# A diffusion backbone on one core: all large SBUF tiles start at multiples of 4096 bytes

## The chip, the cores and the metric

The kernel runs on one core of a Trainium2 chip. The metric is device time in microseconds (us) of one launch. SBUF is the core's working memory: 128 partitions, each with its own row of bytes, and a tile takes the same byte range of every partition. "Offset" means here the byte in a partition at which a tile begins, and "offset modulo 4096" how far past a multiple of 4096 that is.

## The reference

Two layers, each of three sub-layers, run over 256 latent tokens and 256 context tokens of width 1024. Cut to what matters:

```
for l in range(2):
    m = silu(c) @ w_ada[l] + b_ada[l]              # 9 rows of 1024: shift, scale, gate per sub-layer
    x = LN(ALPHA*x + gate * 0.5 * swiglu(modulate(x), ff1_gate, ff1_up, ff1_down))
    h = modulate(x)
    y = concat(neighbourhood_attention(h), rg_lru(h), fourier_mix(h)) @ w_out[l]
    x = LN(ALPHA*x + gate * y)
    x = LN(ALPHA*x + gate * 0.5 * swiglu(modulate(x), ff2_gate, ff2_up, ff2_down))
```

The hidden width of the two feed-forward blocks (FFN) is 2816, and all tensors are float32. Latent and context tokens share all weights. Output: the latent stream, 256 x 1024.

## The kernel before

The activations stand transposed in SBUF, features in the partitions and tokens in the columns: context tokens are columns 0 to 255 and latent tokens 256 to 511. `xT` is the residual stream (8 chunks of 128 features x 512 tokens), `hH` and `hL` the modulated input as a high and a low part, `aH` and `aL` the same for the hidden layer or for the concatenated heads. Splitting into two parts keeps accuracy with the fast matmul type float32r: each product is the sum of three matmuls, high weight x high input, low weight x high input, high weight x low input.

A weight unit is 128 output columns of one matrix over up to 8 blocks of 128 inputs. `issue` (lines 229 to 255) starts its DMA on SyncE's queue into one of five `raw` tiles; each partition receives up to eight pieces of 512 bytes. `use_one` (L257) then has ScalarE cast `raw` to `whi` (L271) and VectorE, at times GpSimd, subtract to get `wlo` (`split_lo`, L583). `mmh` (L383) records every matmul of the projections, in two halves of 256 tokens. The program's names of PSUM targets tell the stage: `gu` is gate and up of an FFN, `dn` its down projection, `pj` the mixer's input projection, `head` the projections that start a sub-layer while its input is still being normalised, `wo` the mixer's output projection, `adat` a small matmul (2 columns) that turns a row of the modulation into columns, `gate` the gates of the recurrence.

The modulation of later sub-layers is computed beside the FFNs by VectorE (`acc`, `fold`, L293 to L299), from `w_ada` blocks that come through the same `raw` tiles. The start (L1209 to L1300) loads `x` and the context into `in` tiles, turns them into `xT` (`xtp`, L1260), and computes the first modulation on TensorE (`adap`, L310). The order of all instructions is written out in the program (nothing is reordered by a scheduler), and each engine runs its own list, waiting on semaphores for the others.

Where tiles lie follows from the order in which they are asked for. The pool `const` holds single tiles, one after the other; behind it follow the pools `wraw` (5 `raw` tiles), `whi`, `wlo` (5 each), `acc` (6), `scr` (13 scratch tiles of 2048 bytes: `s`, `sg`, `pr`, `h32`, ...), `sm` and `dv` (small ones). Every size is rounded up to 32 bytes. The first tile of `const` begins at byte 16512, which is 128 past a multiple of 4096.

Of the kernel before, what the change touches and what calls it, by code (L numbers as in the profile page):

```python
# [11 lines left out]
F32 = mybir.dt.float32  # L12
# [7 lines left out]
DEPTH = 2  # L20
D = 1024
KD = D // 128
# [43 lines left out]
def kernel(ctx: ExitStack, tc: tile.TileContext, x, cx, vecs, cst, bias, w_ada,  # L66
# [3 lines left out]
    const = ctx.enter_context(tc.tile_pool(name="const", bufs=1))  # L70
# [10 lines left out]

    V, S, G, PE = nc.vector, nc.scalar, nc.gpsimd, nc.tensor

    xT = const.tile([128, KD, 512], F32, name="xT")
    hH = const.tile([128, KD, 512], F32R, name="hH")
    hL = const.tile([128, KD, 512], F32R, name="hL")
    aH = const.tile([128, 8, 512], F32R, name="aH")
    aL = const.tile([128, 8, 512], F32R, name="aL")
    cs = const.tile([128, 1408], F32, name="cs")
    ident = cs[:, 0:128]  # L90
    bdC = cs[:, 128:256]
# [1 line left out]
    CN = cs[:, 384:896].rearrange("p (a b) -> p a b", a=2)  # L93
    SN = cs[:, 896:1408].rearrange("p (a b) -> p a b", a=2)
    vT = const.tile([128, V_ROWS], F32, name="vT")
    onesD = const.tile([128, 128], F32, name="onesD")
    one_c = const.tile([128, 1], F32, name="one_c")
    pick = const.tile([128, 2, 2], F32, name="pick")
    scol = const.tile([128, KD, 2], F32, name="scol")
    join = const.tile([128, 2], F32, name="join")  # L100
    bmean = const.tile([128, 6], F32, name="bmean")
    kcol = const.tile([128, 8], F32, name="kcol")
    lbd = const.tile([128, 8, 128], F32, name="lbd")
    fbd = const.tile([128, 2, 128], F32, name="fbd")
    AB = const.tile([128, 2, 2, 128], F32, name="AB")
    scol_z = AB[:, 0].rearrange("p a (k s) -> p (a k) s", s=32)
    mcol = [const.tile([128, 2, 72], F32, name=f"mcol{l}") for l in range(DEPTH)]

    def vcol(name, i, n=1):
        o = V_OFF[name] + i  # L110
# [2 lines left out]
    def s512(nm):  # L113
        return scr.tile([128, 512], F32, tag="s", name=nm)
# [32 lines left out]
    for l in range(DEPTH):  # L147
        p = {}
# [644 lines left out]
    def fno_weights():  # L793
        for c in range(2):
            t = mps("fab")
            PE.matmul(t[:, 0:128], lhsT=bdC, rhs=fbd[:, c], start=True, stop=True)
            PE.matmul(t[:, 128:256], lhsT=bdS, rhs=fbd[:, c], start=True, stop=True)
            S.copy(AB[:, c].rearrange("p a f -> p (a f)"), t[:, 0:256])

# [17 lines left out]
    def mixer(l, both, nm, tl, nxt):  # L817
# [115 lines left out]
        def t_fa(pool, i):  # L933
            t = pool("fa")
            for c in range(2):
                PE.matmul(t[:, c * 256:(c + 1) * 256], lhsT=fT[c][:, i * 128:(i + 1) * 128],
                          rhs=AB[:, c].rearrange("p a f -> p (a f)"), start=True, stop=True)
            fa[i] = s512("fas")
# [461 lines left out]
```

## Time and profile before

| | |
|---|---|
| median of 3 runs | 1828.69 us (1824.31 to 1830.50) |
| the profiled execution | 1825.6 us, span 1823.8 us, mean granted TensorE clock 0.983 |
| TensorE matmul busy | 1746.8 us (96% of the span), 14241 matmuls |
| VectorE busy | 1208.9 us (66%) |
| ScalarE busy | 700.3 us (38%) |
| GpSimd busy | 194.8 us (11%) |
| DMA | 253.33 MB, 139 GB/s in the mean |

Matmuls overlap each other, so a matmul's own duration is longer than its share of the time; the pace is read from how many start in a stretch. The profile names an instruction by its line, engine, and output<-inputs, with buffer numbers left out. The chain of work that ended last is followed back from the last instruction and says which engine the time depended on.

### The profile page before, as it was taken

Reading aid. Unit: us, or ns where it says so; the run is one execution under the profiler, and the core shown is the slowest. Engines: PE = TensorE matmul, PEld = TensorE weight load, DVE = VectorE, ACT = ScalarE, POOL = GpSimd, SP = SyncE. Lnnn points to the kernel's source line nnn. Section 1 sums busy time; section 2 is a strip of 40 time slices with the busy share of each in tenths; the row PEclk is TensorE's granted clock in tenths of the full one; section 3 lists DMA queues with packets and bytes.
Section 4 is the critical chain, followed back from the end, with each engine's and each line's share of the span. In section 5 each row is a group of like instructions: output and inputs, shape, how many; then the busy total and the mean of one; then the engine's idle time right before and its main releaser. Section 6 shows DMA issues by size and latency. Waiting matters only on the chain.

```text
span 1823.8 us, 33834 instructions
## 1 busy us (share of the span) xinstructions
PE 1746.8 (96%) x14241; PEld 1693.7 (93%) x14241; DVE 1208.9 (66%) x1918; ACT 700.3 (38%) x1119; POOL 194.8 (11%) x207
## 2 busy tenths in 40 slices
PE   6999999999989999999999999999999988979997
PEld 4899999998888999999999999999999877869997
DVE  3698879747587488665654669854653758666555
ACT  2232222225856454322222364122122575555443
POOL 1000000005310061000000240000000512040000
PEclk8999999999999999999999999999999999989998
DMA  8565655532222226544453226555653233366662
GB/s 281 171 203 173 182 156 170 172 95 82 70 70 82 70 71 192 157 134 137 139 162 106 82 82 200 173 164 161 192 167 88 79 85 93 92 184 195 177 188 80
DMA packets 375080, 253.33 MB, mean 139 GB/s; under 512 B 8144, under 2 KB 336336, under 8 KB 374928
## 3 DMA queue, kind: packets, MB, share of 16 engines
q1 hardware_dynamic: 373856, 248.81, 46.3%
q8 instruction: 112, 1.84, 0.4%
q0 software_dynamic: 1072, 2.36, 0.4%
q14 instruction: 40, 0.33, 0.1%
HBM read 250.09 MB, written 1.05 MB: 138 GB/s over the span
## 4 chain that ended last, share of the span: by engine, by line
PE 81%; DVE 11%; ACT 5%; issue 2%; DMA 1%; POOL 0%; SPq 0%; DVEq 0%; ACTq 0%
PE gu L383 44%; PE dn L383 22%; PE head L383 5%; PE pj L383 3%; DVE wlo L583 2%; PE wo L383 2%; PE adat L327 2%; ACT whi L271 1%; DVE ri L895 1%; PE o L1089 1%; DVE s L452 1%; DVE xT L710 1%; DVE s L455 1%; PE adap L310 1%; DVE nt L477 1%
## 5 line engine op out<-in xcount | busy, mean ns | idle before, releaser
L383 PE MATMUL gu<-hH,whi 128*128 128x256 f32 x2336 | 498.5, 282 | 1.9 <-ACT hH L1251 1.8
L383 PE MATMUL gu<-hH,wlo 128*128 128x256 f32 x2336 | 495.9, 281 | 1.7 <-DVE wlo L583 1.7
L383 PE MATMUL gu<-hL,whi 128*128 128x256 f32 x2336 | 496.1, 281 | 1.2 <-DVE hL L583 1.1
L583 DVE TENSOR_TENSOR wlo<-raw,whi 128x1024 fp32r<-128x1024 f32 (+1 forms) x296 | 354.2, 1201 | 114.6 <-ACT whi L271 111.2
L271 ACT CAST whi<-raw 128x1024 fp32r<-128x1024 f32 (+1 forms) x319 | 318.7, 1025 | 275.9 <-PE dn L383 102.4
L383 PEld LDWEIGHTS gu<-hH,whi 128*128 128x128 f32 x2336 | 372.4, 190 | 5.9 <-ACT hH L1251 2.5
L383 PEld LDWEIGHTS gu<-hH,wlo 128*128 128x128 f32 x2336 | 372.1, 189 | 2.3 <-DVE wlo L583 2.3
L383 PEld LDWEIGHTS gu<-hL,whi 128*128 128x128 f32 x2336 | 372.4, 190 | 1.7 <-DVE hL L583 1.7
L383 PE MATMUL dn<-aH,whi 128*128 128x256 f32 x1280 | 285.7, 282 | 0.5 <-DVE xT L710 0.5
L383 PE MATMUL dn<-aL,whi 128*128 128x256 f32 x1280 | 283.1, 280 | 0.0
L383 PE MATMUL dn<-aH,wlo 128*128 128x256 f32 x1280 | 283.1, 280 | 0.0
L299 DVE SCALAR_TENSOR_TENSOR acc<-raw,scol,acc 128x512 f32<-128x512 f32 x337 | 236.1, 749 | 1.0
L723 ACT CAST aH<-pr 128x512 fp32r<-128x512 f32 (+1 forms) x88 | 50.0, 568 | 419.5 <-DVE pr L722 419.5
L383 PEld LDWEIGHTS dn<-aH,whi 128*128 128x128 f32 x1280 | 208.2, 188 | 0.8 <-DVE xT L710 0.7
L383 PEld LDWEIGHTS dn<-aH,wlo 128*128 128x128 f32 x1280 | 208.2, 188 | 0.1
L383 PEld LDWEIGHTS dn<-aL,whi 128*128 128x128 f32 x1280 | 208.3, 188 | 0.0
L583 POOL TENSOR_TENSOR wlo<-raw,whi 128x256 fp32r<-128x256 f32 (+2 forms) x55 | 74.2, 1357 | 1143.3 <-ACT whi L271 1134.3
L722 DVE TENSOR_TENSOR pr<-sg,gu 128x512 f32<-128x512 f32 (+1 forms) x84 | 51.6, 614 | 151.0 <-PE gu L383 148.5
L710 DVE SCALAR_TENSOR_TENSOR xT<-dn,gate,xT 128x256 f32<-128x256 f32 x174 | 78.0, 479 | 88.8 <-PE dn L383 88.4
L721 ACT ACTIVATE sg<-gu 128x512 f32<-128x512 f32 (+1 forms) x84 | 45.4, 540 | 117.5 <-PE gu L383 117.3
L383 PE MATMUL pj<-hH,whi 128*128 128x256 f32 x384 | 84.4, 288 | 4.2 <-DVE k L583 2.7
L383 PE MATMUL pj<-hH,wlo 128*128 128x256 f32 x384 | 82.9, 284 | 0.0
(239 smaller groups left out, 2096.3 us busy)
## 6 DMA issues: line engine op xcount, KB each, us to landing
raw<-in_w_ada_dram SPq DMA_DIRECT2D x136, 512.0 KB, 4.6
raw<-in_ff_gate_dram SPq DMA_DIRECT2D x88, 512.0 KB, 4.6
raw<-in_ff_up_dram SPq DMA_DIRECT2D x88, 512.0 KB, 4.7
raw<-in_ff_down_dram SPq DMA_DIRECT2D x64, 448.0 KB, 4.5
raw<-in_w_in_dram SPq DMA_DIRECT2D x36, 512.0 KB, 3.9
raw<-in_ff_down_dram SPq DMA_DIRECT2D x32, 512.0 KB, 4.9
raw<-in_w_out_dram SPq DMA_DIRECT2D x16, 512.0 KB, 4.0
in<-in_w_ada_dram SPq DMA_DIRECT2D x8, 512.0 KB, 7.9
```

The lines of the kernel that those rows point to most:

```text
L271: S.copy(h_[:, :n], t[:, :n])
L299: V.scalar_tensor_tensor(out=a[:, st], in0=t[:, kk * 512:(kk + 1) * 512], scalar=sc_, in1=a[:, st], op0=ALU.mult, op1=ALU.add)
L310: PE.matmul(acc[l, b][32 * (k % 4):32 * (k % 4) + 32, :], lhsT=scol_z[:, k, :], rhs=t[:, kk * 512:(kk + 1) * 512], start=(k < 4), stop=(k ...
L327: PE.matmul(tp[:, q * 2:q * 2 + 2], lhsT=a[:, q * 128:(q + 1) * 128], rhs=w, start=True, stop=True)
L383: PE.matmul(o[:, c], lhsT=w, rhs=X[:, k, c], start=first and i == 0, stop=last and i == len(halves) - 1)
L452: (e1 or V).tensor_tensor(out=s1, in0=a, in1=z, op=ALU.add)
L455: (e2 or V).tensor_tensor(out=s2, in0=b, in1=sq, op=ALU.add)
L583: (eng or V).tensor_tensor(out=dst_l, in0=src, in1=dst_h.bitcast(F32), op=ALU.subtract)
L710: V.scalar_tensor_tensor(out=xT[:, j, a:b], in0=ps[:, a:b], scalar=gate[:, st, j:j + 1], in1=xT[:, j, a:b], op0=ALU.mult, op1=ALU.add)
L721: S.activation(out=sg[:, c], in_=gp[:, c], func=AF.Silu)
L722: V.tensor_tensor(out=pr[:, c], in0=sg[:, c], in1=up[:, c], op=ALU.mult)
L723: S.copy(aH[:, m, c], pr[:, c])
```

## The change

Only the `const` tiles are asked for in another order, with one unused tile of 32 bytes (`pad`) among them. No instruction is added, removed, moved or resized: on each of the five engines the list of instructions with operands, sizes and semaphore waits is the same as before (9084 rows on TensorE, 1782 on VectorE, 1053 on ScalarE, 205 on GpSimd, 488 on SyncE, all equal but for buffer numbers and line numbers).

```diff
+    one_c = const.tile([128, 1], F32, name="one_c")
+    pick = const.tile([128, 2, 2], F32, name="pick")
+    scol = const.tile([128, KD, 2], F32, name="scol")
+    join = const.tile([128, 2], F32, name="join")
+    bmean = const.tile([128, 6], F32, name="bmean")
+    kcol = const.tile([128, 8], F32, name="kcol")
+    mcol = [const.tile([128, 2, 72], F32, name=f"mcol{l}") for l in range(DEPTH)]
+    const.tile([128, 8], F32, name="pad")
+    onesD = const.tile([128, 128], F32, name="onesD")
+    AB = const.tile([128, 2, 2, 128], F32, name="AB")
+    scol_z = AB[:, 0].rearrange("p a (k s) -> p (a k) s", s=32)
     xT = const.tile([128, KD, 512], F32, name="xT")
     hH = const.tile([128, KD, 512], F32R, name="hH")
     hL = const.tile([128, KD, 512], F32R, name="hL")
     aH = const.tile([128, 8, 512], F32R, name="aH")
     aL = const.tile([128, 8, 512], F32R, name="aL")
+    lbd = const.tile([128, 8, 128], F32, name="lbd")
     cs = const.tile([128, 1408], F32, name="cs")
...
     vT = const.tile([128, V_ROWS], F32, name="vT")
-    onesD = const.tile([128, 128], F32, name="onesD")
-    one_c = const.tile([128, 1], F32, name="one_c")
...
-    lbd = const.tile([128, 8, 128], F32, name="lbd")
     fbd = const.tile([128, 2, 128], F32, name="fbd")
-    AB = const.tile([128, 2, 2, 128], F32, name="AB")
...
```

What it does to the offsets, in bytes from the start of a partition (the pools' figure is their first tile; the others follow at steps of the tile's size):

| tile | before | modulo 4096 | after | modulo 4096 |
|---|---|---|---|---|
| xT, hH, hL, aH, aL | 16512, 32896, 49280, 65664, 82048 | 128 | 20480, 36864, 53248, 69632, 86016 | 0 |
| cs (constants, with the identity) | 98432 | 128 | 106496 | 0 |
| lbd (gate weights) | 106336 | 3936 | 102400 | 0 |
| onesD | 105600 | 3200 | 17920 | 1536 |
| AB | 111456 | 864 | 18432 | 2048 |
| raw, whi, wlo, acc | 114656, 135136, 155616, 176096 | 4064 | 114688, 135168, 155648, 176128 | 0 |
| scr (13 x 2048) | 200672 | 4064 and 2016 in turn | 200704 | 0 and 2048 in turn |
| sm, dv | 227296, 228064 | (small) | 227328, 228096 | (small) |

So all that lies behind `const` moves by 32 bytes, and the five large tiles of `const` by 3968. Among `raw`, `whi`, `wlo`, `acc` and `scr` the distances stay as they were.

## Rows read from the trace of the kernel before

**Rows 1.** The page: span, busy time of TensorE, and the DMA queue of SyncE.

```profile
span 1823.8 us, 33834 instructions
PE 1746.8 (96%) x14241; PEld 1693.7 (93%) x14241; DVE 1208.9 (66%) x1918; ACT 700.3 (38%) x1119; POOL 194.8 (11%) x207
...
q1 hardware_dynamic: 373856, 248.81, 46.3%
```

**Rows 2.** The chain that ended last: shares of the span by engine and line.

```profile
PE 81%; DVE 11%; ACT 5%; issue 2%; DMA 1%; POOL 0%; SPq 0%; DVEq 0%; ACTq 0%
PE gu L383 44%; PE dn L383 22%; PE head L383 5%; PE pj L383 3%; DVE wlo L583 2%; PE wo L383 2%; PE adat L327 2%; ACT whi L271 1%; DVE ri L895 1%; PE o L1089 1%; DVE s L452 1%; DVE xT L710 1%; DVE s L455 1%; PE adap L310 1%; DVE nt L477 1%
```

**Rows 3.** The same chain in order of time: start, length, what; five pieces.

```profile
3.18 10.24 DMA in<-in_x_dram
...
191.29 45.16 PE gu L383 x384
...
447.91 18.97 PE head L383 x158
...
815.50 57.07 PE gu L383 x480
...
1691.24 39.42 PE gu L383 x336
```

**Rows 4.** Two stretches: length, busy time by engine, TensorE clock, DMA share, GB/s.

```profile
815.00:873.00 58.00, 58.00 (x492) 58.00 (x491) 32.73 (x44) 15.50 (x20) 0.00 (x0) 1.00 0.45 132
447.00:467.00 20.00, 20.00 (x166) 19.90 (x165) 10.77 (x27) 13.22 (x32) 14.89 (x21) 1.00 0.18 54
```

**Rows 5.** Groups by line and shape: matmuls of L383 (count; busy, mean ns of one).

```profile
L383 PE MATMUL gu<-hH,whi 128*128 128x256 f32 x2336 | 498.5, 282 | 1.9 <-ACT hH L1251 1.8
...
L383 PE MATMUL dn<-aH,whi 128*128 128x256 f32 x1280 | 285.7, 282 | 0.5 <-DVE xT L710 0.5
...
L383 PE MATMUL pj<-hH,whi 128*128 128x256 f32 x384 | 84.4, 288 | 4.2 <-DVE k L583 2.7 <-ACT pt L1058 1.5
...
L383 PE MATMUL head<-hH,whi 128*128 128x256 f32 x256 | 68.0, 297 | 9.4 <-ACT hH L597 8.8 <-ACT hH L595 0.7
...
L383 PE MATMUL wo<-aH,whi 128*128 128x256 f32 x144 | 34.6, 286 | 0.0
```

**Rows 6.** The same view: weight loads from tiles at three different offsets.

```profile
L383 PEld LDWEIGHTS gu<-hH,wlo 128*128 128x128 f32 x2336 | 372.1, 189 | 2.3 <-DVE wlo L583 2.3
...
L871 PEld LDWEIGHTS gate<-xl,lbd 128*128 128x128 f32 x32 | 5.8, 190 | 7.5 <-issue 4.0 <-PE gate L871 1.6 <-ACT ri L872 1.5
...
L1277 PEld LDWEIGHTS mean<-xT,onesD 128*128 128x128 f32 x16 | 3.0, 190 | 4.2 <-issue 4.2
```

**Rows 7.** Timeline of TensorE, matmuls of two columns: the last five, and the last three.

```profile
190.48 0.70 PE L327 MATMUL adat<-pick,fold 128*128 128x2 f32 x5
...
190.70 0.47 PE L327 MATMUL adat<-pick,fold 128*128 128x2 f32 x3
```

**Rows 8.** Groups by line and shape: two-input VectorE operations on SBUF alone.

```profile
L583 DVE TENSOR_TENSOR wlo<-raw,whi 128x1024 fp32r<-128x1024 f32 x235 | 287.9, 1230 | 94.2 <-ACT whi L271 91.7 <-issue 1.9
...
L583 DVE TENSOR_TENSOR aL<-pr,aH 128x512 fp32r<-128x512 f32 x66 | 45.0, 685 | 4.8 <-ACT aH L723 4.8
...
L351 DVE TENSOR_TENSOR fold<-fold 128x512 f32<-128x512 f32 x24 | 16.4, 684 | 0.0
...
L452 DVE TENSOR_TENSOR s<-s,xT 128x512 f32<-128x512 f32 x12 | 8.3, 692 | 0.4
```

**Rows 9.** The same view: ScalarE casts at two sizes from each side.

```profile
L271 ACT CAST whi<-raw 128x1024 fp32r<-128x1024 f32 x255 | 260.6, 1046 | 237.3 <-PE dn L383 96.1 <-DMA raw<-in_ff_gate_dram 50.6 <-DMA raw<-in_ff_up_dram 34.9
...
L723 ACT CAST aH<-pr 128x512 fp32r<-128x512 f32 x66 | 41.0, 621 | 365.0 <-DVE pr L722 365.0
...
L595 ACT CAST hH<-h 128x256 fp32r<-128x256 f32 x63 | 25.6, 407 | 2.0
```

**Rows 10.** Windows: the stretch of the start in which the inputs land.

```profile
4.00:14.00 10.00, 3.10 (x11) 1.66 (x10) 1.12 (x6) 0.22 (x1) 4.86 (x9) 1.00 1.01 357
```

More of the change, by code (lines that the diff above doesn't have):

```diff
@@ L95 @@
     vT = const.tile([128, V_ROWS], F32, name="vT")
-    onesD = const.tile([128, 128], F32, name="onesD")
-    one_c = const.tile([128, 1], F32, name="one_c")
[L98 to L102, printed above, removed]
-    lbd = const.tile([128, 8, 128], F32, name="lbd")
     fbd = const.tile([128, 2, 128], F32, name="fbd")
-    AB = const.tile([128, 2, 2, 128], F32, name="AB")
-    scol_z = AB[:, 0].rearrange("p a (k s) -> p (a k) s", s=32)
-    mcol = [const.tile([128, 2, 72], F32, name=f"mcol{l}") for l in range(DEPTH)]
     def vcol(name, i, n=1):
```

## The prediction, on record before the changed kernel ran

> **What bounds the kernel now.** I read the page first: TensorE is busy 1746.8 of 1823.8 us, 96% [rows 1]. Then the chain that ended last: 81% of the span hangs on TensorE, 11% on VectorE, 5% on ScalarE and 1% on DMA, and the line of the projection matmuls, L383, alone makes up 44 + 22 + 5 + 3 + 2 = 76% [rows 2]. The reader is to see that a change of tile addresses can matter much only if it changes the pace of those matmuls. So I went to the chain in order of time, where a long piece of matmuls without a gap gives their pace: 45.16 us for 384 is 117.6 ns each, 39.42 for 336 is 117.3, 57.07 for 480 is 118.9, 18.97 for 158 is 120.1 [rows 3]. The granted clock was 1.00 in both of the slower two [rows 4], so the differences are not the clock's. Nor are they load from other engines: the piece at 118.9 ns ran beside a VectorE busy 32.73 of 58 us and an idle GpSimd, the one at 120.1 beside a GpSimd busy 14.89 of 20 us and with a smaller DMA share [rows 4], and the fastest pace occurs in the middle of an FFN with all its transfers. I take 117.8 ns as the mean (between 117.3 and 118.9). There are 2336 + 1280 + 384 + 256 + 144 = 4400 matmuls in the first operand pair of each stage, and three pairs of each: 13,200 [rows 5]. At 117.8 ns that is 1555 us, 85% of the span.
>
> **The change part by part.** It removes, adds and moves no instruction and no wait, and every transfer keeps its queue, its place and its size. Only offsets change. Each engine's work therefore has one question: does the duration of an operation depend on the offset of its operands? The trace of before holds no large tile at a multiple of 4096, but it holds operands at 128, 864, 3200, 3936, 2016 and 4064 modulo 4096, so a dependence has had occasions to show.
>
> *TensorE, weights.* Loads from `wlo` (offset 4064) take 189 ns, from `lbd` (3936) 190 and from `onesD` (3200) 190 [rows 6]. No dependence: zero. *TensorE, moving data.* All L383 matmuls read `hH`, `hL`, `aH` or `aL` at 128 modulo 4096, so no row compares two offsets there directly, and I bound the price from both sides. Below: the `adat` matmuls move 2 columns in place of 256, and each still takes its own weight load. Two of them lie between the rows that begin with five and with three left, 0.22 us apart in start and 0.23 in length, so 110 to 115 ns, say 112, each [rows 7]. Whatever the reading of the 256 columns adds to the pace is then 117.8 - 112 = 5.8 ns at most; were it all due to the offset, 13,200 x 5.8 ns = 77 us would go. Above: the slowest pace that the trace shows is 120.1, so 2.3 ns more on each, 30 us. I take zero: the two largest groups read from different tiles and both take 282 ns [rows 5], and the pace moves between 117.3 and 120.1 from stretch to stretch with the offsets unchanged, so what sets it there is not the offset.
>
> *VectorE.* Operations of 512 columns with two SBUF inputs take 685 ns (`pr` at 4064 or 2016 with `aH` and `aL` at 128), 684 (`fold`, all at 4064) and 692 (`s` at 4064 or 2016 with `xT` at 128) [rows 8]. The spread is 8 ns in 688, 1.2%; on the 11% of the span that hangs on VectorE, 201 us, that is 2.4 us either way. The three operands of `wlo` are at the same offset as each other before and after. I take zero. [...] The rows agree, 684 against 685 and 692 ns; the only case that they do not hold is the offset of 0 itself.
>
> *ScalarE.* From 256 to 512 columns a cast goes from 407 to 621 ns, 0.836 ns a column, with the output at 128 modulo 4096; carried on to 1024 columns this gives 1049, and `whi<-raw`, with both operands at 4064, takes 1046 [rows 9]. 3 ns in 1046 on the 5% of the chain, 91 us, is 0.3 us. Zero.
>
> *DMA.* SyncE's queue keeps the 16 DMA engines busy 46.3% of the span [rows 1], but the chain holds DMA for 1%, and its one long piece is the landing of `x` at the start, 10.24 us [rows 3]. There the DMA share is 1.01 at 357 GB/s [rows 10], so the engines are the limit for those 10 us. Below: even if that wait vanished, 10.24 us would go. Above: with all other DMA waits hidden behind TensorE, a loss of the same third that I grant as a gain below, 3.4 us. I take zero: the largest pieces of this stretch are rows of 4 KB and 2 KB, where a start off by 32 bytes is a small share of the piece.
>
> The sum is zero: 1825.6 us for the profiled execution stays as it is. That execution lies 3.1 us under the median of the runs, 1828.69; the forecast for the median is **1828.5 us**.
>
> **The rivals.**
>
> *A: the moving data is read faster from aligned tiles.* A half of 256 columns is 1024 bytes and begins at 128 past a multiple of 1024 before and at a multiple after, and a weight block of 512 bytes likewise no longer straddles a multiple of 512. If straddling costs part of each matmul, the pace drops toward 112 ns. For it: TensorE carries 81% of the chain, and 5.8 ns a matmul are unexplained by the weight load. Against it: the loads at three offsets agree, and pace steps occur with offsets fixed. In full it gives 1828.7 - 77 = 1752 us; half of it 1790. It decides from 0.4 ns a matmul, which is 5.5 us.
>
> *B: slower, because weights and moving data now meet at the same offset.* Before, a weight block and the moving chunk that it meets lie 160 bytes apart modulo 512; after, both begin at a multiple of 512. If the two reads of a matmul get in each other's way when they start at equal low address bits, TensorE falls to a slower one of the paces that the trace shows: 118.9 everywhere is 1.1 ns x 13,200 = 14.5 us, 1843 us; 120.1 everywhere is 30 us, 1859 us. For it: such slower paces exist, at full clock. Against it: `raw`, `whi` and `wlo` share one offset already and VectorE and ScalarE read and write them at the same speed as mixed ones. It decides from 0.4 ns a matmul.
>
> *C: transfers get shorter.* Each 512-byte piece of a weight lands at 224 past a multiple of 256 before and at 0 after. If a landing that straddles costs extra, DMA share falls from 46.3%, but time only where the chain holds DMA: a third of 10.24 us is 3.4 us, 1825.3 us; all of it, 1818.5. Against it: the row at the start is mostly larger pieces, and elsewhere the waits for `raw` end on ScalarE (50.6 and 34.9 us of idle time, [rows 9]), which the chain does not show as DMA time. [...]
>
> *D: the change does not do what it says.* The offsets of the built programs, in the table above, exclude it.
>
> **How the numbers follow.** No change in any term: 0.73. A: 0.11. B: 0.10. C: 0.06. What a measurement of this kernel can tell from no change is about 0.3%, 5.5 us; its own runs lie 6.2 us apart. Of the 0.79 in which nothing or C happens I give 0.05 to a result that looks faster by over 0.3%, and 0.03 to one that looks slower. Faster: 0.11 + 0.05 = 0.16; slower: 0.10 + 0.03 = 0.13; the same: 0.71. The likeliest case by itself spans 1822 to 1835 (the spread of the runs, 6.2 us, about the median). To hold 8 in 10 the range goes down to C's full price, 1818, and up to 1840, which takes in the VectorE bound of 2.4 us and a partial B; it leaves out A and the greater part of B, under 0.2 together.
>
> **What the profile would show.** Right: long pieces of `gu` and `dn` on the chain again at 117.3 to 120.1 ns, mean durations 282 and weight loads 189; `wlo` near 1230, `whi` near 1046; the chain's shares as before within a point. A would show as long pieces under 117 ns; B as most long pieces at 118.9 or above; C as a DMA share clearly under 46.3% with the same bytes, and the landing of `x` before 13.4 us. The forecast is wrong if an operation has a price that begins or ends exactly at a multiple of 1024 or 4096, a case that no row of before holds.

## The result: 1.1% slower, and the profile after

| | before | changed |
|---|---|---|
| median of the runs | 1827.63 us (4 runs, 1824.31 to 1830.5) | 1846.96 us (4 runs, 1846.34 to 1848.82) |
| ratio | | 1.0108, 95% interval 1.0089 to 1.0128 |
| profiled execution | 1825.6 us, span 1823.8 | 1846.34 us, span 1844.5 |

The forecast was 1828.5 us and no change, with a range of 1818 to 1840. The time lies above the range, on rival B's side, between its two prices of 1843 and 1859 us. The page of the changed kernel, busy times and the shares of the chain, answers to [rows 1, 2]:

```profile
span 1844.5 us, 33834 instructions
PE 1770.8 (96%) x14241; PEld 1717.4 (93%) x14241; DVE 1210.4 (66%) x1918; ACT 699.7 (38%) x1119; POOL 194.9 (11%) x207
...
q1 hardware_dynamic: 373856, 248.81, 45.0%
...
PE 82%; DVE 10%; ACT 5%; issue 2%; DMA 1%; POOL 0%; SPq 0%; DVEq 0%; ACTq 0%
```

TensorE has the same 14,241 matmuls and is busy 24.0 us longer (1770.8 against 1746.8); the span grew by 20.7. VectorE, ScalarE and GpSimd moved by 1.5 us or less. Next the chain in order of time (start, length, what), with the pieces that answer to [rows 3]:

```profile
3.17 9.51 DMA in<-in_x_dram
...
57.89 47.59 PE gu L385 x382
...
190.46 46.18 PE gu L385 x384
...
427.08 2.42 DVE mod L573
...
451.21 18.97 PE head L385 x158
...
821.11 57.70 PE gu L385 x480
...
1709.40 40.32 PE gu L385 x336
```

The 384 matmuls now take 46.18 us, the 480 take 57.70, the 336 take 40.32: 120.3, 120.2 and 120.0 ns each, where it was 117.6, 118.9 and 117.3. Only the 158 of `head`, which already stood at 120.1, did not move. Before, several paces alternated; now there is one, and it is the slowest of the old ones. The windows over the two stretches that answer to [rows 4] have these lines (length, busy time by engine, TensorE clock, DMA share, GB/s):

```profile
821.00:879.00 58.00, 58.00 (x486) 58.00 (x486) 32.73 (x44) 15.49 (x20) 0.00 (x0) 1.00 0.43 132
451.00:470.00 19.00, 19.00 (x159) 18.97 (x159) 10.78 (x27) 12.72 (x30) 13.93 (x20) 1.00 0.20 57
```

The granted clock is 1.00 in both, as before, and VectorE, ScalarE and DMA do the same work beside the matmuls. So the pace changed with nothing beside it changed but the addresses. The groups by line and shape answer to [rows 5, 6, 8, 9]:

```profile
L385 PE MATMUL gu<-hH,whi 128*128 128x256 f32 x2336 | 503.6, 285 | 1.9 <-ACT hH L1253 1.8
...
L385 PEld LDWEIGHTS gu<-hH,wlo 128*128 128x128 f32 x2336 | 378.3, 193 | 2.1 <-DVE wlo L585 2.1
...
L585 DVE TENSOR_TENSOR wlo<-raw,whi 128x1024 fp32r<-128x1024 f32 x235 | 288.0, 1230 | 94.5 <-ACT whi L273 91.6 <-issue 2.2
L585 DVE TENSOR_TENSOR aL<-pr,aH 128x512 fp32r<-128x512 f32 x66 | 45.0, 685 | 4.8 <-ACT aH L725 4.8
L353 DVE TENSOR_TENSOR fold<-fold 128x512 f32<-128x512 f32 x24 | 16.4, 685 | 0.0
```

A matmul's mean record goes from 282 to 285 ns and a weight load's from 189 to 193. VectorE's three groups stand where they stood, 1230, 685 and 685 against 1230, 685 and 684.

**Where the 20.7 us of span lie.** Landmarks that both chains hold cut the span into parts: the first long piece of `gu` (60.02 before, 57.89 after), the `mod` operations that open the mixers (424.02 and 427.08; 1425.71 and 1440.95), the one that ends the first mixer (643.91 and 648.17), the piece of 144 `gu` that opens the last FFN (1622.36 and 1638.88), and the last piece of `dn` (1808.41 and 1829.10). The start ends 2.1 us earlier; in before the granted clock was 0.84 from 40 to 60 us, in after 1.00 from 40 to 58. Those 2.1 us are not shown to belong to the change: in the experiments below the first long piece begins at 57.82 to 59.15 us in the other kernels at the distance of the changed one, and at 58.08 and 58.91 in the others at the distance of before. The first FFN takes 5.2 us more (369.19 against 364.0), the two FFNs between the mixers 11.0 (792.78 against 781.8), the last 4.2 (190.22 against 186.05), the mixers 1.2 and 1.3, the tail nothing. So the FFNs, the stages with the dense matmuls, lost 20.3 us, the mixers 2.5, and the start gave back 2.1.

### The profile page after: what moved, and what is told of

It is laid out like the page before. It is cut to its first block, busy times and chain, and to the rows that moved or that the text cites. A ratio compares the mean times of both kernels' runs of the same rounds, so it can differ in the third digit from the quotient of the medians.

```text
span 1844.5 us, 33834 instructions
## 1 busy us (share of the span) xinstructions
PE 1770.8 (96%) x14241; PEld 1717.4 (93%) x14241; DVE 1210.4 (66%) x1918; ACT 699.7 (38%) x1119; POOL 194.9 (11%) x207
## 4 chain that ended last, share of the span: by engine, by line
PE 82%; DVE 10%; ACT 5%; issue 2%; DMA 1%; POOL 0%; SPq 0%; DVEq 0%; ACTq 0%
PE gu L385 46%; PE dn L385 22%; PE head L385 5%; PE pj L385 3%; PE wo L385 2%; DVE wlo L585 2%; PE adat L329 2%; ACT whi L273 1%; DVE ri L897 1%; PE o L1091 1%; DVE xT L712 1%; DVE s L457 1%; PE adap L312 1%; DVE nmx L1026 1%; DVE s L454 1%
## 5 line engine op out<-in xcount | busy, mean ns | idle before, releaser
L385 PE MATMUL gu<-hH,whi 128*128 128x256 f32 x2336 | 503.6, 285 | 1.9 <-ACT hH L1253 1.8
L385 PEld LDWEIGHTS gu<-hH,whi 128*128 128x128 f32 x2336 | 378.5, 193 | 5.8 <-ACT hH L1253 2.5
L385 PEld LDWEIGHTS gu<-hH,wlo 128*128 128x128 f32 x2336 | 378.3, 193 | 2.1 <-DVE wlo L585 2.1
L385 PEld LDWEIGHTS gu<-hL,whi 128*128 128x128 f32 x2336 | 378.5, 193 | 1.7 <-DVE hL L585 1.7
L385 PEld LDWEIGHTS dn<-aH,whi 128*128 128x128 f32 x1280 | 212.0, 192 | 1.3 <-DVE xT L712 1.2
L385 PEld LDWEIGHTS dn<-aH,wlo 128*128 128x128 f32 x1280 | 212.1, 192 | 0.1
L385 PEld LDWEIGHTS dn<-aL,whi 128*128 128x128 f32 x1280 | 212.1, 192 | 0.0
```

The costliest lines, as they stand in the source:

```text
L385: PE.matmul(o[:, c], lhsT=w, rhs=X[:, k, c], start=first and i == 0, stop=last and i == len(halves) - 1)
```

## The experiments

Three theories stood at first. **R** (rival B): what counts is the distance between moving data (`hH`, `hL`, `aH`, `aL`) and weights (`whi`, `wlo`) modulo some power of two. **M**: aligned moving data is slow by itself. **W**: aligned weights are slow by themselves. Below, r is the offset of the moving data minus that of the weights, modulo 256: 160 before, 0 after. Every kernel of this section has all 34 thousand instructions of before, and only offsets differ. A pace is a long piece of the chain divided by its matmuls; the same two pieces are used throughout, `gu` x384 of the first FFN and `gu` x336 of the last. The kernel before ran beside the experiments, with medians of 1828.32, 1829.37, 1827.33, 1828.48 and 1828.01 us in the five sets. Where no number of runs is given a kernel ran once; before itself came out anywhere from 1822.37 to 1830.43 us in eight runs, so a difference in time of less than 8 us says little by itself, and the paces carry the argument. Windows over these pieces give a granted clock of 1.00 for both pieces of before and of the changed kernel and inside the piece of 336 at r = 192; over the whole profiled executions the mean granted clock of the 18 kernels lies between 0.979 and 0.986, and the fastest kernel has the lowest.

### First set: moving data, weights, or the distance

*128 and 0 (r = 128)*, from before: the weights go to a multiple of 4096, the moving data stays.

```diff
     mcol = [const.tile([128, 2, 72], F32, name=f"mcol{l}") for l in range(DEPTH)]
+    const.tile([128, 8], F32, name="pad0")
```

> Moving data (hH, hL, aH, aL) at 128 modulo 4096 as before, weights (raw, whi, wlo) and scratch at 0 as after. Theory W (weights at a multiple of 4096 slow the matmuls): 120.0 ns a matmul in all long pieces, about 1847 us. Theory M (moving data at a multiple of 1024 does) and theory R (weights and moving data at equal offsets do): long pieces between 117.3 and 118.9 ns, about 1828 us.

*0 and 96 (r = 160)*, from the changed kernel: the moving data stays aligned, the distance goes back to that of before.

```diff
     fbd = const.tile([128, 2, 128], F32, name="fbd")
+    const.tile([128, 24], F32, name="pad1")
```

> Moving data at 0 modulo 4096 as after, weights and all behind them at 96. Theory M: 120.0 ns and about 1847 us. Theories W and R: between 117.3 and 118.9 ns, about 1828 us.

*224 and 224 (r = 0)*, from the changed kernel: nothing is aligned, the distance stays 0.

```diff
-    const.tile([128, 8], F32, name="pad")
```

> The changed kernel without its 32-byte pad: moving data and weights both at 4064, so neither is at a multiple of 4096, but both begin at the same offset. Theory R: 120.0 ns and about 1847 us. Theories M and W: between 117.3 and 118.9 ns, about 1828 us.

*160 and 0 (r = 160)*, from before: weights aligned, the distance of before.

```diff
+    const.tile([128, 8], F32, name="pad0")
     xT = const.tile([128, KD, 512], F32, name="xT")
```

> The kernel before with one pad of 32 bytes in front of all tiles: all offsets move by 32, moving data to 160 and weights to 0, their distance stays 160. Theory W: 120.0 ns, about 1847 us. Theories M and R: between 117.3 and 118.9 ns, about 1828 us. If the pace were an accident of each layout that no offset explains, this run need not agree with the kernel before.

Measured: 1835.02 (128 and 0), 1827.59 (0 and 96), 1845.55 (224 and 224) and 1829.36 us (160 and 0). The chain of the second (0 and 96), in order of time:

```profile
189.87 45.17 PE gu L386 x384
...
814.00 57.07 PE gu L386 x480
...
1692.05 39.87 PE gu L386 x336
```

and of the third (224 and 224):

```profile
190.38 46.18 PE gu L384 x384
...
820.47 57.70 PE gu L384 x480
...
1708.54 40.32 PE gu L384 x336
```

With moving data at a multiple of 4096 but r = 160, the paces of before return, 117.6 and 118.9 ns (before had 45.16 and 57.07 for the same pieces). With nothing aligned but r = 0, the slow pace is there in full, to 0.01 us. With the weights aligned but r = 160 the time is that of before, 1829.36 us. M and W fall, and R stands: 4096 itself plays no part. The new distance, 128, stands between: 1835.02 us, and 118.7 ns in the piece of 336.

### Second set: the period and the shape

If R holds, the distance has a period and perhaps a better value. Here small tiles are asked for behind `fbd` in place of ahead of `xT`, which sets r in steps of 32 bytes. The diffs of this set, and *r = 32* and *r = 96* below, are against the changed kernel.

*256 modulo 512, so 0 modulo 256*:

```diff
-    pick = const.tile([128, 2, 2], F32, name="pick")
-    scol = const.tile([128, KD, 2], F32, name="scol")
-    join = const.tile([128, 2], F32, name="join")
-    bmean = const.tile([128, 6], F32, name="bmean")
-    kcol = const.tile([128, 8], F32, name="kcol")
-    const.tile([128, 8], F32, name="pad")
     fbd = const.tile([128, 2, 128], F32, name="fbd")
+    pick = const.tile([128, 2, 2], F32, name="pick")
+    scol = const.tile([128, KD, 2], F32, name="scol")
+    join = const.tile([128, 2], F32, name="join")
+    bmean = const.tile([128, 6], F32, name="bmean")
+    kcol = const.tile([128, 8], F32, name="kcol")
+    const.tile([128, 16], F32, name="pad0")
```

> Distance 256: moving data begins 256 bytes past the weights modulo 512 (288 against 32). If the pace follows the distance modulo 256: 120.0 ns, about 1846 us, as at distance 0. If it follows the distance modulo 512: another pace, and by the nearest case (distance 160, 117.3 and 118.6 ns) about 1829 us.

*480 modulo 512 (r = 224)*: `kcol` alone moves.

```diff
-    kcol = const.tile([128, 8], F32, name="kcol")
-    const.tile([128, 8], F32, name="pad")
     fbd = const.tile([128, 2, 128], F32, name="fbd")
+    kcol = const.tile([128, 8], F32, name="kcol")
```

> Distance 480, that is moving data 32 bytes ahead of the weights modulo 512. If only equal offsets collide: 117.3 to 118.6 ns and about 1828 us. If nearness counts: 119 to 120 ns and 1840 to 1847 us.

*448 modulo 512 (r = 192)*: the same with `bmean` too.

```diff
-    bmean = const.tile([128, 6], F32, name="bmean")
-    kcol = const.tile([128, 8], F32, name="kcol")
-    const.tile([128, 8], F32, name="pad")
     fbd = const.tile([128, 2, 128], F32, name="fbd")
+    bmean = const.tile([128, 6], F32, name="bmean")
+    kcol = const.tile([128, 8], F32, name="kcol")
```

> Distance 448, moving data 64 bytes ahead of the weights modulo 512. If only equal offsets collide: 117.3 to 118.6 ns, about 1828 us. If multiples of 64 are the bad ones (distance 128 had 118.6 throughout): 118.6 or 120.0 ns, 1835 us or more.

*320 modulo 512 (r = 64)*: as the first of this set, without its last line.

```diff
-    const.tile([128, 16], F32, name="pad0")
```

> Distance 320, half a period of 512 and 64 more. If multiples of 64 are bad: 118.6 or 120.0 ns, 1835 us or more. If the pace is a matter of how far the two are apart within 512: 117.3 ns in most long pieces, 1822 to 1829 us.

Measured: 1847.68, 1832.10, 1817.71 and 1819.33 us. The chain at 256 modulo 512:

```profile
190.22 46.18 PE gu L385 x384
...
1710.75 40.32 PE gu L385 x336
```

and at 448 modulo 512:

```profile
185.98 45.33 PE gu L384 x384
...
579.64 10.90 PE pj L384 x96
...
1683.19 39.57 PE gu L384 x336
```

256 is as slow as 0, 120.0 ns for the 336, so the period is 256 bytes, not the 512 that rival B named (0 and 96 in the first set stands at 416 modulo 512 and had the paces of 160; a period of 128 is out, since r = 128 had 118.7). At 192 and 64 the long pieces go at 117.8 ns, and a short piece of `pj` at 113.5 (10.90/96): a pace that no long piece of before has. Of the times expected only that for 256 was met: 480 came out between its two cases, and 448 and 320 were faster than either of theirs.

### Third set: which tiles, and more distances

*r = 32* and *r = 96*, in each the small tiles that now stand behind `fbd`; ahead of `onesD` they and `pad` are gone:

```diff
     fbd = const.tile([128, 2, 128], F32, name="fbd")
+    one_c = const.tile([128, 1], F32, name="one_c")
+    pick = const.tile([128, 2, 2], F32, name="pick")
+    scol = const.tile([128, KD, 2], F32, name="scol")
+    join = const.tile([128, 2], F32, name="join")
+    bmean = const.tile([128, 6], F32, name="bmean")
+    kcol = const.tile([128, 8], F32, name="kcol")
+    mcol = [const.tile([128, 2, 72], F32, name=f"mcol{l}") for l in range(DEPTH)]
+    const.tile([128, 32], F32, name="pad0")
```

> Distance 32 modulo 256 (moving data at 128, weights at 96). Theory R says only that it is not 120.0 ns. If the curve over the distance is symmetric about 128, as the equal paces at 64 and 192 suggest, it behaves like distance 224: 118.3 ns in most long pieces, about 1832 us.

```diff
     fbd = const.tile([128, 2, 128], F32, name="fbd")
+    one_c = const.tile([128, 1], F32, name="one_c")
+    pick = const.tile([128, 2, 2], F32, name="pick")
+    join = const.tile([128, 2], F32, name="join")
+    bmean = const.tile([128, 6], F32, name="bmean")
+    kcol = const.tile([128, 8], F32, name="kcol")
```

> Distance 96 modulo 256 (352 modulo 512). If the curve is symmetric about 128, it behaves like distance 160: a mixture of 117.3 and 118.7 ns, about 1829 us. If lower distances are in general better than higher ones: 117.7 ns or less, about 1819 us.

*A gap of 64 bytes in the changed kernel*, once ahead of `whi` (then `whi` and `wlo` lie at 64 and `raw` stays at 0), once behind `wlo` (then only `acc` and the scratch tiles move). The edit is the same but for the place of the pool:

```diff
+    gap = ctx.enter_context(tc.tile_pool(name="gap", bufs=1))
...
+    gap.tile([128, 16], F32, name="gap")
```

> The changed kernel with 64 bytes left free between raw and whi: moving data and raw stay at multiples of 4096, and whi, wlo and all behind them begin at 64. If it is the weights that TensorE loads which must not meet the moving data: 117.7 ns as at distance 192, about 1818 us. If raw (landings, reads of ScalarE and VectorE) against the moving data is what counts: 120.0 ns, about 1847 us.

> The changed kernel with the 64 bytes left free behind wlo instead: moving data, raw, whi and wlo stay at multiples of 4096, only acc and the scratch tiles begin at 64. If the weights against the moving data count: 120.0 ns, about 1847 us. If the scratch tiles of VectorE and ScalarE against the moving data count: below 119 ns and 1835 us or less.

Measured: r = 32 1817.67 us, r = 96 1847.12, gap ahead of `whi` 1818.45, gap behind `wlo` 1847.84. The chain at r = 96:

```profile
191.22 46.19 PE gu L384 x384
...
1710.17 40.32 PE gu L384 x336
```

and with the gap ahead of `whi`:

```profile
189.17 45.33 PE gu L387 x384
...
1116.67 21.88 PE gu L387 x192
...
1683.95 39.57 PE gu L387 x336
```

64 bytes ahead of `whi` give back all that the change cost and 9 us more; the same 64 bytes behind `wlo` give nothing. So the effect lies between the matmuls' own two operands; `raw`, `acc` and the scratch tiles have no part in it. Two guesses of mine fell here: that distances mirror each other (96 would equal 160, 32 would equal 224), and that lower distances are in general better than higher ones, since 96 is as slow as 0.

### Fourth and fifth set: the two weight tiles apart, and the times in rounds

Of each three matmuls two read `whi` and one `wlo`. *Split 192 and 64*: the layout of r = 192, with 128 bytes between `whi` and `wlo`, so r = 192 for one and 64 for the other.

```diff
+    gap = ctx.enter_context(tc.tile_pool(name="gap", bufs=1))
...
+    gap.tile([128, 32], F32, name="gap")
```

> Two distances in one kernel: whi at 192 and wlo at 64 modulo 256, both of which alone gave 117.7 ns and, in some stretches, 113.3. If each matmul pays for its own pair of weights and moving data: 117.7 ns, about 1818 us. If the pace is a lock between successive matmuls that a change of distance breaks: other paces, either below 115 ns (under 1800 us) or above 118 ns.

*Split 64 and 32*: the layout of r = 64, with 32 bytes between the two.

```diff
+    gap.tile([128, 8], F32, name="gap")
```

> whi at distance 64, wlo at 32 modulo 256. If each matmul pays for its own pair: between 116.7 and 117.7 ns, about 1817 us. If the lock between successive matmuls decides: other paces, either below 115 ns (under 1800 us) or above 118 ns.

*r = 176*: the layout of r = 192, with the four moving tiles as slices of one tile that begin 16 bytes into it. The expectation says 208, and that is wrong: the one tile is 32 bytes longer than the four were, so all that lies behind it moves as well. `hH` begins at 36784 and `whi` at 135168, which makes the distance 176; its neighbours are 160 and 192, not 192 and 224.

```diff
+    quad = const.tile([128, 4 * 4096 + 8], F32R, name="quad")
+    hH, hL, aH, aL = (quad[:, 4 + i * 4096:4 + (i + 1) * 4096].rearrange("p (k n) -> p k n", k=8) for i in range(4))
```

> hH, hL, aH and aL are slices of one tile that begin 16 bytes in, so the distance is 208 modulo 256, between 192 (117.7 ns) and 224 (118.3 ns). If the unit of the effect is 32 bytes: as one of these two, 1818 to 1832 us. If 16-byte offsets count: a pace outside 117.7 to 118.3 ns.

*r = 32, timed in three rounds:*

> The kernel of distance 32 again, now timed in rounds against the kernel before. If its pace of 116.7 to 117.7 ns belongs to the distance and not to one execution: 1815 to 1820 us, ratio 0.993 to 0.996, interval clear of 1.

*Split 0 and 128*: the layout 224 and 224 of the first set, with 128 bytes between `whi` and `wlo`; whether the split alone makes the fast pace.

```diff
+    gap.tile([128, 32], F32, name="gap")
```

> whi and wlo again 128 bytes apart modulo 256, but at distances 0 and 128 from the moving data. If it is the 128 bytes between whi and wlo that gave 113.3 ns: 113.3 ns again, about 1780 us. If what counts is the distance from the moving data: 118.7 to 120.0 ns, 1835 to 1847 us.

*Split 192 and 64, timed in three rounds:*

> The kernel with whi at distance 192 and wlo at 64 again, timed in rounds against the kernel before. If its pace of 113.3 ns belongs to the offsets and not to one execution: 1777 to 1783 us, ratio 0.971 to 0.976, interval clear of 1.

Measured: split 192 and 64 1779.61 us; split 64 and 32 1834.66; r = 176 1841.13; split 0 and 128 1833.62. In rounds, r = 32 took 1816.29 us (5 runs, 1815.61 to 1817.17), 0.9943 of before [0.9923, 0.9963], and split 192 and 64 took **1779.94 us** (4 runs, 1778.72 to 1780.62), **0.9736 of before [0.9719, 0.9754]**. The chain of the last, and the window over its piece of 480:

```profile
186.86 43.65 PE gu L386 x384
...
796.14 54.53 PE gu L386 x480
...
1648.94 38.08 PE gu L386 x336
```

```profile
797.00:850.00 53.00, 53.00 (x470) 53.00 (x469) 31.92 (x42) 15.50 (x20) 0.00 (x0) 1.00 0.49 145
```

113.7, 113.6 and 113.3 ns, at the same clock of 1.00 and with the same engines at work beside it. The page shows what the faster TensorE leaves behind:

```profile
PE 79%; DVE 13%; ACT 5%; issue 2%; DMA 1%; SPq 0%; DVEq 0%; ACTq 0%
```

VectorE's share of the chain rises from 11 to 13%: 13,200 matmuls by 4.5 ns (117.8 to 113.3) are 59 us, and 48 of them arrive (1828.01 to 1779.94).

The same pieces of split 64 and 32:

```profile
191.60 45.76 PE gu L386 x384
...
1699.89 39.57 PE gu L386 x336
```

of r = 176:

```profile
192.33 45.90 PE gu L382 x384
...
1704.94 40.07 PE gu L382 x336
```

and of split 0 and 128:

```profile
191.16 45.62 PE gu L386 x384
...
1697.43 40.03 PE gu L386 x336
```

All distances together; the last two columns are the pieces of 384 (us, and ns each) and of 336:

| kernel | r of `whi` / `wlo` | time, us | x384 | x336 |
|---|---|---|---|---|
| changed | 0 / 0 | 1846.96 | 46.18, 120.3 | 40.32, 120.0 |
| 224 and 224 | 0 / 0 | 1845.55 | 46.18, 120.3 | 40.32, 120.0 |
| 256 modulo 512 | 0 / 0 | 1847.68 | 46.18, 120.3 | 40.32, 120.0 |
| gap behind `wlo` | 0 / 0 | 1847.84 | 46.17, 120.2 | 40.32, 120.0 |
| r = 32 | 32 / 32 | 1816.29 | 44.91, 117.0 | 39.20, 116.7 |
| r = 64 | 64 / 64 | 1819.33 | 45.33, 118.0 | 39.57, 117.8 |
| r = 96 | 96 / 96 | 1847.12 | 46.19, 120.3 | 40.32, 120.0 |
| 128 and 0 | 128 / 128 | 1835.02 | 45.67, 118.9 | 39.87, 118.7 |
| before | 160 / 160 | 1827.63 | 45.16, 117.6 | 39.42, 117.3 |
| 0 and 96 | 160 / 160 | 1827.59 | 45.17, 117.6 | 39.87, 118.7 |
| 160 and 0 | 160 / 160 | 1829.36 | 45.17, 117.6 | 39.87, 118.7 |
| r = 176 | 176 / 176 | 1841.13 | 45.90, 119.5 | 40.07, 119.3 |
| r = 192 | 192 / 192 | 1817.71 | 45.33, 118.0 | 39.57, 117.8 |
| gap ahead of `whi` | 192 / 192 | 1818.45 | 45.33, 118.0 | 39.57, 117.8 |
| r = 224 | 224 / 224 | 1832.10 | 45.54, 118.6 | 39.76, 118.3 |
| split 192 and 64 | 192 / 64 | 1779.94 | 43.65, 113.7 | 38.08, 113.3 |
| split 64 and 32 | 64 / 32 | 1834.66 | 45.76, 119.2 | 39.57, 117.8 |
| split 0 and 128 | 0 / 128 | 1833.62 | 45.62, 118.8 | 40.03, 119.1 |

Kernels with the same pair of distances agree to 0.13% however their tiles lie. Three things follow from the rest. First, a distance allows several paces. At 160 the piece of 336 stands at 117.3 in one kernel and at 118.7 in two others. It is not the layout that chooses: the kernel of r = 32 ran twice under the profiler, and its piece of 480 took 56.64 us (118.0 ns) in one execution and 56.11 (116.9) in the other:

```profile
810.95 56.64 PE gu L385 x480
```

```profile
811.60 56.11 PE gu L385 x480
```

In before a stretch keeps the pace with which it begins: from one start of a matmul to the next, the pieces of 384 and 336 have a mean of 117.3 ns in each full 60 matmuls, and the piece of 480 one of 118.7 or 118.8 until its last 60. Second, a pace isn't the mean of what each matmul pays for its own pair: 192 and 64 give 117.8 each, together 113.3, and 64 and 32, both good alone, give 1834.66 us, worse than either. The other reading in those two expectations, a lock between successive matmuls, was a guess of mine that no run shows, and split 64 and 32 has 117.8 in its last FFN, which that reading did not foresee. Third, the split as such is not the cause: 0 and 128 stay at 118.8 and 119.1.

## Why the prediction was wrong

**The step that failed** is the second half of "*TensorE, moving data*": "I take zero: [...] the pace moves between 117.3 and 120.1 from stretch to stretch with the offsets unchanged, so what sets it there is not the offset." The observation was right, the conclusion wrong, and with it the term that the sum put at zero: it measured 2.0 ns a matmul. At r = 160 paces of 117.3, 118.7 and 120.1 are all possible, and at r = 0 only 120.0, in long pieces. That something varies while an input is fixed does not show that the input is without effect; it can still decide between which values it varies. The first half has the same flaw: that two groups which read different tiles both take 282 ns says nothing when all four tiles lie at the same distance from the weights.

**Rival B named the right thing**, the place of the weights against that of the moving data, at a chance of 0.10. Three of its details were off. The period is 256, not 512. "When they start at equal low address bits" is not the condition, since a distance of 96 is as slow as 0. And "120.1 everywhere is 30 us, 1859 us" is too much. From one matmul's start to the next, where nothing holds them up, the mean over the projections went from 117.9 to 120.0 ns, 2.0 ns on 13,200 matmuls or 27 us; the FFNs passed on 20.3 of it and the mixers 2.5, and the start came 2.1 us earlier, which leaves the 20.7 us of span. Where the other 4 us went into waits is not shown. B's sign, most long pieces at 118.9 ns or above, is what the profile showed. The argument against it, that VectorE and ScalarE are indifferent to operands at one offset, was true and beside the point: those rows hold no matmul.

**Weight loads: "No dependence: zero"** compared offsets modulo 4096 of tiles that differ in what they are multiplied with. In the changed kernel the same loads take 193 ns in place of 189.

**VectorE and ScalarE, zero:** right. `wlo` 1230 and 1230, `whi` 1046 and 1044, `aL` 685 and 685, `fold` 684 and 685 ns. The offset of 0, the one case that the rows before did not hold, has no price there.

**DMA, zero:** right for the time, though the transfers did get a little shorter. Both signs that the prediction named for C appeared: the share fell from 46.3 to 45.0%, and the landing of `x` ended at 12.68 us, after 9.51 us in place of 10.24. In the trace of before, with `raw` at 224 modulo 256, the 324,096 packets of 512 bytes on the queue take 28.6 ns in the mean; in that of the changed kernel, with `raw` at a multiple of 256, 28.0. That is C's direction, at 2% of a packet and not the third that it was granted, and the time does not follow it: at r = 0, `raw` at 224 gives 1845.55 us and `raw` at 0 gives 1846.96 and 1847.84. The landing of `x` shows no such order: 9.51 to 10.65 us where its `in` tiles begin at a multiple of 256, 9.84 to 10.32 where they begin at 224.

**A, the moving data read faster from aligned tiles:** fell. Its bound of 112 ns from the two-column matmuls was sound all the same: 113.3 ns is the fastest pace that a long piece of any run showed, reached by two distances and not by alignment.

**What stays open.** The runs show that the pace hangs on the two distances modulo 256; of the other tiles, `raw`, `acc` and scratch were moved apart from them, without effect. Why it hangs on them no run shows. Why 96 is as bad as 0, why the pair 192 and 64 is good, and what decides which of its paces a stretch takes are not explained. Nor is it known whether r = 176 is slow for its distance or because its moving data begins 16 bytes off a multiple of 32, as in no other kernel; 18 layouts are no full map, and a better one may exist.

## What to carry to other kernels

Where matmuls with a weight load each run back to back, read the pace from long pieces of the chain and try a few distances between weights and moving data modulo 256 bytes, for each weight tile by itself: a pad of 32 to 128 bytes moved this kernel between 1780 and 1847 us. Aligning every large tile to 4096 bytes set both distances to 0, which was, with 96, the slowest found (1846.96 and 1847.12 us). And when a pace moves between a few values with nothing changed, ask what allows those values and no others before calling any input irrelevant.

## What the runs showed of the hardware

A 128x256 fp32r matmul with its own weight load came every 113.3 to 120.0 ns in the piece of 336, 6% from end to end, with nothing changed but where its operands lie: 113.3 at 192 and 64, 117.8 at r = 192, 120.0 at r = 0. The granted clock was 1.00 in that piece in before and in the changed kernel, inside it at r = 192, and inside the piece of 480 of split 192 and 64. The slices at 176, 16 bytes from r = 192, gave 119.3. The trace shows the pace and the offsets, and not what in the chip ties the one to the other.
